# Hybrid decoder layer on one core: block sums of weights in two parts, stores of accumulated tiles from GpSimd's queue, p and x loaded at other steps

## The chip, the core and the metric

The kernel runs on one core of a Trainium2 chip. A core has TensorE (PE, matmuls; its weight loads are listed as PEld), VectorE (DVE), ScalarE (ACT), GpSimd (POOL) and SyncE (SP), each with its own instruction queue in program order, and 16 DMA engines. Here SP issues nearly all DMAs, and POOL issues those that add in flight to a tile. The metric is the device time of one execution in microseconds, and a comparison goes by the median of several.

## What is computed

One decoder layer on x of 1024 x 1024 in float32: half an FFN, two attention mixers with gates, half an FFN, and a gated embedding of p. What matters here:

```python
def rms_norm(x, g):
    xf = x.astype(jnp.float32)
    y = xf * lax.rsqrt(jnp.mean(xf * xf, axis=-1, keepdims=True) + EPS)
    return (y * g.astype(jnp.float32)).astype(x.dtype)

def swiglu(h, w_gate, w_up, w_down):
    return (jax.nn.silu(h @ w_gate) * (h @ w_up)) @ w_down

    x = x + 0.5 * swiglu(rms_norm(x, ffn1_norm[i]), ffn1_w_gate[i], ffn1_w_up[i], ffn1_w_down[i])
    h = rms_norm(x, mix_norm[i])
    ...   # y_fox, y_sb: forgetting and stick-breaking attention on h @ w_in
    merged = (jax.nn.sigmoid(g_fox) * (y_fox @ w_branch_fox[i])
              + jax.nn.sigmoid(g_sb) * (y_sb @ w_branch_sb[i]))
    x = x + merged @ w_out[i]
    x = x + 0.5 * swiglu(rms_norm(x, ffn2_norm[i]), ffn2_w_gate[i], ffn2_w_up[i], ffn2_w_down[i])
    x = x + jax.nn.sigmoid(rms_norm(x, ple_norm[i]) @ w_ple_gate[i]) * (p[i] @ w_ple_proj[i])
```

D_MODEL and SEQ are 1024, D_FF is 2816, PLE_DIM is 256.

## The kernel before

**Products.** Every float32 operand is split into a high and a low part, and a product is three passes (high by high, and the two mixed ones) of four 128-deep matmuls: 12 matmuls of 128x512, all recorded at line 613. `make_up` multiplies the normed activations with weight blocks of 256 columns. Both are cut in two by two, and instead of eight block products it forms seven, of sums and differences, as Strassen's scheme does. Product (n, m) is number m of weight block n. Block 0 alone is done plainly, with eight (`plain`).

**Operands of the weights.** `part(n, m)` names the weight operand of (n, m): four quarters of the two raw tiles `r[0]` and `r[1]`, and sums of them. `sums(n)` (lines 573 to 578) makes three, of 128x512 each, and `last_sum(n)` (line 581) a fourth. `prep(n, m)` splits an operand: ScalarE casts the high part and another engine, VectorE as a rule, subtracts for the low part (line 106 of the helper `split`, the cast is line 105). In the steady blocks POOL makes the sums, at the start of a stage VectorE.

**Operands of the activations.** `combo_a` to `combo_u`, `combo_s`, `combo_d` and `combo_e` form the seven activation operands B[m]; in each, `high` is a cast on ScalarE (line 645) and `low` a subtraction on VectorE (line 649). `combo_s(j, 7)` writes B[7], read by the products (n, 7). `combo_d(j)` (lines 727, 728 or 730) prepares and `combo_e(j)` writes B[4], read by (n, 4). In the first FFN the activations come by rows (`rows()` is true) and each d is two operations.

**Order.** `make_up` is used in four stages: first FFN, gates (in `mix_start`, evictions at lines 1311 to 1325), second FFN, and PLE (`ple_start`, lines 1700 to 1773). Within them the order of each engine's instructions is that of the program text, and a reader waits through semaphores for what it reads or overwrites. Step s of a stage is: product number s of `up_order`, its `evict` from PSUM, `begin(s)`, and `prep` of the product four steps later. The list begins (2,1), (1,5), (2,2), (1,6), (1,7), (2,6), (2,5), (1,3), (2,7), (1,4), (3,1), (2,4), (3,2); PLE, with four blocks, ends (3,6), (3,5), (3,7), (2,3), (3,3), (3,4). Products 1, 6, 7 and 4 of a block add up in one bank of PSUM, and 6 and 7 are each copied out by ScalarE (lines 776 and 778 in the FFNs, 1313 and 1315 in the gates, 1732 and 1734 in PLE). (1,6) and (1,7) are neighbours; in later blocks another product stands between 6 and 7.

**Slots.** Tiles come from tagged slots ("T" six, "Q" two, "KH" two, "WH" three, and so on). A load into a slot waits in its issuing queue until the last reader of the tile before is done.

**PLE.** `pd` holds p @ w_ple_proj and `xe` the residual, both in DRAM. After the sigmoid, `finish(n, i)` multiplies the tile E[n][i] with p's (line 1714), then either POOL issues a DMA that adds x to the tile (line 1716) or VectorE adds a loaded tile of x (line 1718), and the tile is stored (line 1719). `fetch` loads p, or p and x (line 1709). The table `AT` says behind which step each is done.

Of the kernel before, what the change touches and what calls it, by code (L numbers as in the profile page):

```python
# [14 lines left out]
ALU = mybir.AluOpType  # L15
# [3 lines left out]
P = 128  # L19
# [17 lines left out]
def tile_hybrid_decoder_layer(  # L37
# [6 lines left out]
    nc = tc.nc  # L44
# [7 lines left out]
    def nm(s):  # L52
        uid[0] += 1
        return f"{s}_{uid[0]}"

    def slot(tag, shape, dt=F32):
        pad = -shape[-1] % 16
        t = sb.tile([*shape[:-1], shape[-1] + pad], dt, tag=tag, bufs=BUFS[tag], name=nm(tag))
        return t[:, :, :shape[-1]] if pad else t
# [29 lines left out]
    def f(ap):  # L89
        return ap.bitcast(F32)  # L90
# [71 lines left out]
    pd = dp.tile([KD, P, S], F32, name="p_proj")  # L162
# [27 lines left out]
    def norm_sum(N, ps):  # L190

        acc = N.pop("acc")
        for t in range(4):
            pe(nc.tensor.matmul(ps[:, t:t + 1], acc[:, t * P:(t + 1) * P], ones1[:], start=True, stop=True))  # L194
        norm_pow(N, ps)
# [175 lines left out]
    def up_first(N, F):  # L371

        F.load(2)
        F.prep(0, 5)
        F.prep(0, 4)
        F.plain(0, 0, (0, 1), False)
        norm_sum(N[1], bank("sc"))
        F.prep(1, 1)
        F.prep(1, 2)
        F.sums(1, nc.vector)  # L380
        F.silu(0, 0)
        F.prep(1, 5)
        F.plain(1, 0, (0,))
        norm_row(N[1], bank("av"))
        F.plain(1, 0, (1,), False)
        combos(F)
        F.silu(1, 0)
        products(F)
# [144 lines left out]
    def make_up(N, src, nm_, tags, first_fn, first_done=None, over=None):  # L533

        B = {}
        W, hls, E = {}, {}, {}
# [7 lines left out]
        def part(n, m):  # L544
            r = W[n]["r"]
            one, two = slice(0, P), slice(P, 256)
            if m in (6, 7):
                return W[n]["s"][:, 7 - m]
            return {1: r[0][:, :, one], 5: r[0][:, :, two], 2: r[1][:, :, one], 3: r[1][:, :, one], 4: r[1][:, :, two]}[m]

        def plain(f_, half, parts=(0, 1), out=True):

# [17 lines left out]
            if first_done is not None and half:  # L570
                first_done(0, f_, E[0][f_])

        def sums(n, eng=nc.gpsimd):
            W[n]["s"] = slot(tags["sum"].get(n, "RAW"), [P, 2, 4, P])
            a11, a21, a22, s3, s2 = part(n, 1), part(n, 5), part(n, 4), part(n, 7), part(n, 6)
            eng.tensor_sub(s3, a11, a21)
            eng.tensor_add(a21, a21, a22)
            eng.tensor_sub(s2, a21, a11)

        def last_sum(n, eng=nc.gpsimd):  # L580
            eng.tensor_sub(part(n, 2), part(n, 2), part(n, 6))
# [46 lines left out]
        def rows():  # L628
            return "rows" in N[0]
# [95 lines left out]
        def combo_d(j):  # L725
            if rows():
                nc.vector.tensor_sub(w(j, 0), f(cut(B[2], 0, j)), w(j, 1))
                nc.vector.tensor_add(w(j, 0), w(j, 0), f(cut(B[2], 1, j)))
            else:
                nc.vector.tensor_sub(w(j, 0), h0(j, 1), w(j, 1))  # L730

        def combo_e(j):
            if j == 0:
                B[4] = home(4)
            high(4, j, w(j, 0))
            low(4, j, w(j, 0))

        def begin(s):

            if s == 0:  # L740
                for q in range(4):
                    combo_s(q, 7)
            elif s == 1:
                sums(2, nc.vector)
            elif s == 2:
                last_sum(1, nc.vector)
                last_sum(2, nc.vector)
            if rows():
                if 1 < s < 6:
                    combo_d(s - 2)  # L750
            elif 0 < s < 3:
                combo_d(2 * s - 2)
                combo_d(2 * s - 1)
            if 2 < s < 7:
                combo_e(s - 3)
        return types.SimpleNamespace(a=combo_a, b=combo_b, t=combo_t, l=combo_l, u=combo_u, s=combo_s, load=load, prep=prep, sums=sums, last_sum=last_sum, plain=plain, silu=silu, product=product, begin=begin, E=E, B=B, bank_of=bank_of)

    def ffn(N, wg, wu, wd, resid, hid, tags, entry, tail):
# [360 lines left out]
    pend, late = [], []  # L1119
# [489 lines left out]
    tags = {"raw": {1: ("KH", "KL")}, "sum": {}, "w": ("Q", "Q", "KH", "KL"), "hl": ("WL", "WL", "WL", "WH") + ("PT",) * 4 + ("WL", "WL", "WL", "PT"), "B": {"12": "X", 3: ("T",) * 4, 5: "H", 6: "H", 7: "X", 4: "X"}}  # L1609
# [10 lines left out]
    xe = dp.tile([KD, P, S], F32, name="x_end")  # L1620
# [79 lines left out]
    def ple_start():  # L1700

        N, Xs, T = [], [], {}
        tags_p = {"raw": UP_TAGS["raw"], "sum": UP_TAGS["sum"], "hl": UP_TAGS["hl"], "cycle": ("WL", "WL", "WL", "PT", "PT", "PT"),
                  "B": {"12": "H", 3: "H", 5: "X", 6: ("T",) * 4, 7: "H", 4: "X"}}

        def fetch(n, i, *tags):
            r = T[n, i] = [slot(tag, [P, 2, 512]) for tag in tags]
            for t, src in zip(r, (pd, xe)):
                nc.sync.dma_start(t[:], src[2 * n + i].rearrange("p (h n) -> p h n", h=2))

        def finish(n, i, h=slice(0, 2), cols=slice(0, 512), add_in_dma=True):

            e = E[n][i][:, h, cols]
            nc.vector.tensor_mul(e, e, T[n, i][0][:, h, cols])
            if add_in_dma:
                nc.gpsimd.dma_start(e, xe[2 * n + i].rearrange("p (h n) -> p h n", h=2)[:, h, cols], accum_op=ALU.add)
            else:
                nc.vector.tensor_add(e, e, T[n, i][1][:, h, cols])
            nc.sync.dma_start(out[0, (2 * n + i) * P:(2 * n + i + 1) * P, :].rearrange("p (h n) -> p h n", h=2)[:, h, cols], e)

        F = make_up(N, lambda n: kp(w_ple_gate[0])[:, :, n * 256:n * 256 + 256], 4, tags_p, AF.Sigmoid)
        E = F.E
        h0, h1 = slice(0, 1), slice(1, 2)

        def evict(n, m, ps):
            if m == 1:
                E[n] = [slot(t, [P, 2, 512]) for t in (("Y", "Y") if n == 2 else ("GF", "RN"))]
            e1, e2 = E[n]
            if m == 1:
                nc.scalar.copy(e1[:, 0, :], ps[:])  # L1730
            elif m == 6:
                nc.scalar.copy(e1[:, 1, :], ps[:])  # L1732
            elif m == 7:
                nc.scalar.copy(e2[:, 1, :], ps[:])
                nc.vector.tensor_add(e2[:, 1, :], e2[:, 1, :], F.bank_of[n, "d"][:])  # L1735
                nc.scalar.activation(e2[:, 1, :], e2[:, 1, :], AF.Sigmoid)
            elif m == 2:
                nc.vector.tensor_add(e1[:, 0, :], e1[:, 0, :], ps[:])
                if n == 3:
                    nc.scalar.activation(e1[:, 0, :], e1[:, 0, :], AF.Sigmoid)  # L1740
            elif m == 3:
                nc.vector.tensor_add(e1[:, 1, :], e1[:, 1, :], ps[:])
                hs = h1 if n == 3 else slice(0, 2)
                nc.scalar.activation(e1[:, hs], e1[:, hs], AF.Sigmoid)
            elif m == 4:
                nc.scalar.activation(e2[:, 0, :], ps[:], AF.Sigmoid)
        F.evict = evict
        late = (slice(0, 512), False)
        AT = {4: [(fetch, 0, 1, "Q"), (finish, 0, 0)], 6: [(finish, 0, 1), (fetch, 1, 0, "KH"), (fetch, 1, 1, "KH")], 8: [(fetch, 2, 1, "T")],
              9: [(finish, 1, 0)], 10: [(fetch, 3, 0, "Q", "Q")], 11: [(finish, 1, 1), (fetch, 2, 0, "KH", "KH")], 12: [(fetch, 3, 1, "T", "T")],  # L1750
              13: [(finish, 2, 1)], 14: [(finish, 3, 0, h0)], 16: [(finish, 3, 1, h1, *late)], 17: [(finish, 2, 0, slice(0, 2), *late), (finish, 3, 0, h1, *late)]}

        def begin(i, X):
            if not Xs:
                Xs.extend(X)
            up_begin(N, X, 2, F, i)

        def end():
            fetch(0, 0, "T")
            up_first(N, F)  # L1760
            seqn = up_order(4)
            for s, (n, m) in enumerate(seqn[:-1]):
                evict(n, m, F.product(n, m))
                F.begin(s)
                if s + 4 < len(seqn):
                    F.prep(*seqn[s + 4])
                for fn, *args in AT.get(s, ()):
                    fn(*args)
            for cols in (slice(0, 256), slice(256, 512)):
                ps = F.product(3, 4, cols)  # L1770
                nc.scalar.activation(E[3][1][:, 0, cols], ps[:, cols], AF.Sigmoid)  # L1771
                finish(3, 1, h0, cols, False)
        return types.SimpleNamespace(begin=begin, step=lambda i, t: up_step(N, Xs, xe, F, i, t), end=end)
# [36 lines left out]
```

## Time and profile before

| | |
|---|---|
| median of 3 runs | 2266.73 us (2263.55 to 2269.24) |
| the profiled execution | 2264.37 us, span 2262.6 us, granted clock 0.995 |
| PE busy | 2217.6 us, 98% of the span |
| DVE, ACT, POOL busy | 67%, 44%, 36% |
| start of step 0: first FFN, gates, second FFN, PLE | 47.3, 684.8, 1551.7, 2190.2 us |

The page of the profile gives busy times, and beside a group of instructions the idle time just before them and what ended it. In the timeline a row is: start in us, length in us, engine, line, operation, output and inputs by the program's names, count, and in brackets the idle time before it and its releaser. Rows of one kind that follow each other are merged (x24). The ends of matmuls are modelled, so a row of 12 is listed with 2.88 us though the next may start 2.72 us after it. Rows of POOLq and SPq are queues that issue DMAs; the time to landing runs from the issue.

### The profile page before, as it was taken

The page shows a single profiled execution, that of the slowest core. Times are in us where ns is not written, and L with a number is a line of the kernel's source. Part 1 is how long each engine was busy: PE and PEld are TensorE (multiplying, and loading weights), DVE is VectorE, ACT ScalarE, POOL GpSimd, SP SyncE. Part 2 cuts the span into 40 slices and gives each one's busy share as a digit, 9 for nine tenths or more (in the row PEclk, how much of TensorE's full clock was granted, in tenths as well). Part 3 has the DMA queues.
Part 4 walks back from the last instruction along what each step waited for, and adds up shares of the span by engine and source line. Part 5 has one row for each costly group of instructions (what it writes and reads, how often), then busy time and mean ns, then how long its engine had stood idle before and what let it go on. Part 6 is the DMA issues. An engine that isn't in the chain of part 4 may idle for free. (4 is left out here: it accounts for less than half of the span.)

```text
span 2262.6 us, 30509 instructions
## 1 busy us (share of the span) xinstructions
PE 2217.6 (98%) x11210; PEld 1884.4 (83%) x11210; DVE 1511.6 (67%) x2365; ACT 1005.6 (44%) x1805; POOL 817.4 (36%) x788
## 2 busy tenths in 40 slices
PE   9999999999999999999999999999999999999997
PEld 7788888888887899999898888887888888888876
DVE  8755555588887325666678775788554545778895
ACT  6333333333354445555566663255333333433453
POOL 1344444300021336565567664420544444200111
PEclk9999999999999999999999999999999999999998
DMA  4232323384323333233323366641423232754427
GB/s 140 93 126 84 126 80 130 135 320 172 112 93 112 119 119 109 85 113 85 84 66 90 107 196 233 237 162 40 135 93 117 86 124 84 268 197 167 136 69 228
DMA packets 196328, 298.30 MB, mean 132 GB/s; under 512 B 28746, under 2 KB 108874, under 8 KB 196179
## 3 DMA queue, kind: packets, MB, share of 16 engines
q1 hardware_dynamic: 195312, 293.47, 39.1%
q0 software_dynamic: 864, 2.88, 0.8%
q8 instruction: 88, 1.44, 0.3%
q14 instruction: 62, 0.50, 0.1%
q10 hardware_dynamic: 2, 0.00, 0.0%
HBM read 196.40 MB, written 83.13 MB: 124 GB/s over the span
## 5 line engine op out<-in xcount | busy, mean ns | idle before, releaser
L509 PE MATMUL ps<-H,H 128*128 128x512 f32 x2184 | 497.2, 390 | 0.0
L509 PEld LDWEIGHTS ps<-H,H 128*128 128x128 f32 x2184 | 409.8, 188 | 84.5
L613 PE MATMUL ps<-H,WL 128*128 128x512 f32 x1164 | 276.9, 391 | 2.9 <-ACT GF L1732 2.9
L613 PEld LDWEIGHTS ps<-H,WL 128*128 128x128 f32 x1164 | 219.6, 189 | 48.7 <-ACT GF L1732 3.3
L185 POOL TENSOR_TENSOR PT<-PT,PT 128x512 f32<-128x512 f32 x27 | 35.0, 1294 | 405.7 <-ACT PT L182 404.9
L613 PE MATMUL ps<-X,WL 128*128 128x512 f32 (+1 forms) x588 | 140.2, 388 | 12.4 <-ACT RN L1771 9.2
L613 PE MATMUL ps<-H,Q 128*128 128x512 f32 x624 | 148.4, 389 | 0.0
L517 DVE SCALAR_TENSOR_TENSOR X<-ps,X 128x512 f32<-128x512 f32 x168 | 110.2, 686 | 47.4 <-PE ps L509 47.3
L613 PEld LDWEIGHTS ps<-X,WL 128*128 128x128 f32 x588 | 110.1, 191 | 35.0 <-ACT RN L1771 9.4
L613 PEld LDWEIGHTS ps<-H,Q 128*128 128x128 f32 x624 | 117.2, 188 | 24.2
L613 PE MATMUL ps<-H,PT 128*128 128x512 f32 x540 | 129.1, 390 | 0.7 <-DVE RN L1735 0.7
L139 POOL TENSOR_TENSOR WL<-RAW,WH 128x512 fp32r<-128x512 f32 (+1 forms) x84 | 97.4, 1180 | 67.4 <-ACT WH L129 43.2
L1214 DVE TENSOR_TENSOR PT<-ps,PT 128x512 fp32r<-128x512 f32 (+1 forms) x160 | 100.0, 627 | 31.9 <-ACT PT L1208 31.1
L613 PEld LDWEIGHTS ps<-H,PT 128*128 128x128 f32 x540 | 101.3, 188 | 22.1 <-DVE RN L1735 1.1
L891 PE MATMUL ps<-WH,H 128*128 128x256 f32 x768 | 116.2, 288 | 0.8 <-ACT RN L956 0.8
L899 PE MATMUL ps<-H,WH 128*128 128x512 f32 x384 | 115.0, 407 | 0.0
L1232 PE MATMUL ps<-PT,X 128*128 128x256 f32 (+1 forms) x640 | 102.6, 286 | 6.8 <-DVE PT L1214 5.6
L1208 ACT CAST PT<-ps 128x512 fp32r<-128x512 f32 (+1 forms) x160 | 87.1, 548 | 43.1 <-PE ps L1206 40.5
L1232 PEld LDWEIGHTS ps<-PT,X 128*128 128x128 f32 x640 | 90.4, 190 | 17.3 <-DVE PT L1214 10.4
L891 PEld LDWEIGHTS ps<-WH,H 128*128 128x128 f32 x768 | 101.4, 190 | 2.7 <-ACT RN L956 1.2
L412 POOL TENSOR_TENSOR PT<-GF,RN 128x512 f32<-128x512 f32 x20 | 33.6, 1682 | 188.5 <-DVE GF L799 188.5
L1160 POOL TENSOR_TENSOR T<-T,l 128x128 f32<-128x128 f32 (+3 forms) x64 | 73.2, 1146 | 72.5 <-DVE l L1159 70.4
(439 smaller groups left out, 4782.2 us busy)
## 6 DMA issues: line engine op xcount, KB each, us to landing
hidden<-PT SPq DMA_DIRECT2D x40, 512.0 KB, 2.6
WH<-in_ffn_w_gate_dram SPq DMA_DIRECT2D x38, 512.0 KB, 4.9
Q<-hidden SPq DMA_DIRECT2D x24, 512.0 KB, 5.7
hidden<-RN SPq DMA_DIRECT2D x22, 512.0 KB, 2.9
KH<-in_ffn_w_up_dram SPq DMA_DIRECT2D x20, 512.0 KB, 6.2
KL<-in_ffn_w_up_dram SPq DMA_DIRECT2D x20, 512.0 KB, 6.9
T<-in_ffn_w_down_dram SPq DMA_DIRECT2D x20, 512.0 KB, 6.6
GF<-hidden SPq DMA_DIRECT2D x14, 512.0 KB, 7.4
```

What stands on the lines that cost most here:

```text
L139: ins = eng_lo.tensor_sub(lo[part], raw[part], f(hi[part]))
L185: add = lambda eng: eng.tensor_add(N["acc"], N["acc"], d)
L412: eng.tensor_add(s12[:, 0, :], g1[:, 1, :], g2[:, 1, :])
L509: pe(nc.tensor.matmul(groups[g][t][:], wt[:, b, k, t * P:(t + 1) * P], act[:, a, k, :], start=(fresh and n == 0), stop=(i in (6, 1, 4) and ...
L517: nc.vector.scalar_tensor_tensor(xs, groups[g][t][:], scale, xs, ALU.mult, ALU.add)
L613: pe(nc.tensor.matmul(ps[:, cols], hl[:, a, k, :], right(B[m], b, k)[:, cols], start=(first and i == 0), stop=(final and i == 11), skip_gr ...
L891: pe(nc.tensor.matmul(ps[:, :n], hT[t // 4](a, k)[:, (t % 4) * P:(t % 4 + 1) * P], w[k // 4][b][:, k % 4, :n], start=(i == 0), stop=(i == ...
L899: pe(nc.tensor.matmul(ps[:], w[a][:, k, :], hT[half](b, k), start=(i == 0), stop=(i == 23)))
L1160: nc.gpsimd.tensor_mul(T[:, :n], T[:, :n], l[:].broadcast_to([P, n]))
L1208: high = nc.scalar.copy(pt[:, 0, :width], ps[:, :width])
L1214: ins = nc.vector.tensor_sub(pt[:, 1, :width], ps[:, :width], f(pt[:, 0, :width]))
L1232: pe(nc.tensor.matmul(o, lh, r, start=(kpair == c and i == 0), stop=(kpair == 0 and i == 3)))
```

## The change

`sums` now writes a21 + a22 to the first half of a slot and that sum less a11 to the second, and the third sum, a11 - a21, is a function of its own, `third_sum`, done in place in the raw tile. For block 2 the first two are made at step 0 ahead of `combo_s` (all three were made at step 1), the third at step 3, and `last_sum(2)` at step 7 (it was at step 2). Where the rows are not used, d is done at steps 2 and 3 (it was 1 and 2); e is done at steps 4 to 7 everywhere (it was 3 to 6). In PLE a store that follows an adding DMA is issued by POOL and no longer by SP, each `fetch` loads one tile, and the steps and slots of the loads are others.

```diff
@@ make_up
         def part(n, m):
             r = W[n]["r"]
             one, two = slice(0, P), slice(P, 256)
-            if m in (6, 7):
-                return W[n]["s"][:, 7 - m]
-            return {1: r[0][:, :, one], 5: r[0][:, :, two], 2: r[1][:, :, one], 3: r[1][:, :, one], 4: r[1][:, :, two]}[m]
+            if m == 6 or m == 5 and "s" in W[n]:
+                return W[n]["s"][:, m - 5]
+            return {1: r[0][:, :, one], 5: r[0][:, :, two], 7: r[0][:, :, two], 2: r[1][:, :, one], 3: r[1][:, :, one], 4: r[1][:, :, two]}[m]
...
-        def sums(n, eng=nc.gpsimd):
+        def sums(n, eng=nc.gpsimd, split_=False):
+            a21 = part(n, 5)
             W[n]["s"] = slot(tags["sum"].get(n, "RAW"), [P, 2, 4, P])
-            a11, a21, a22, s3, s2 = part(n, 1), part(n, 5), part(n, 4), part(n, 7), part(n, 6)
-            eng.tensor_sub(s3, a11, a21)
-            eng.tensor_add(a21, a21, a22)
-            eng.tensor_sub(s2, a21, a11)
+            eng.tensor_add(part(n, 5), a21, part(n, 4))
+            eng.tensor_sub(part(n, 6), part(n, 5), part(n, 1))
+            if not split_:
+                third_sum(n, eng)
+
+        def third_sum(n, eng):
+            eng.tensor_sub(part(n, 7), part(n, 1), part(n, 7))
...
         def begin(s):

             if s == 0:
+                sums(2, nc.vector, True)
                 for q in range(4):
                     combo_s(q, 7)
-            elif s == 1:
-                sums(2, nc.vector)
             elif s == 2:
                 last_sum(1, nc.vector)
+            elif s == 3:
+                third_sum(2, nc.vector)
+            elif s == 7:
                 last_sum(2, nc.vector)
-            if rows():
-                if 1 < s < 6:
-                    combo_d(s - 2)
-            elif 0 < s < 3:
-                combo_d(2 * s - 2)
-                combo_d(2 * s - 1)
-            if 2 < s < 7:
-                combo_e(s - 3)
+            for j in range(4):
+                if s == (j + 2 if rows() else 2 + j // 2):
+                    combo_d(j)
+            if 3 < s < 8:
+                combo_e(s - 4)
@@ ple_start
-        def fetch(n, i, *tags):
-            r = T[n, i] = [slot(tag, [P, 2, 512]) for tag in tags]
-            for t, src in zip(r, (pd, xe)):
-                nc.sync.dma_start(t[:], src[2 * n + i].rearrange("p (h n) -> p h n", h=2))
+        def fetch(n, i, tag, x=False):
+            t = T[(n, i, "x") if x else (n, i)] = slot(tag, [P, 2, 512])
+            nc.sync.dma_start(t[:], (xe if x else pd)[2 * n + i].rearrange("p (h n) -> p h n", h=2))

         def finish(n, i, h=slice(0, 2), cols=slice(0, 512), add_in_dma=True):

             e = E[n][i][:, h, cols]
-            nc.vector.tensor_mul(e, e, T[n, i][0][:, h, cols])
+            nc.vector.tensor_mul(e, e, T[n, i][:, h, cols])
+            queue = nc.gpsimd if add_in_dma else nc.sync
             if add_in_dma:
-                nc.gpsimd.dma_start(e, xe[2 * n + i].rearrange("p (h n) -> p h n", h=2)[:, h, cols], accum_op=ALU.add)
+                queue.dma_start(e, xe[2 * n + i].rearrange("p (h n) -> p h n", h=2)[:, h, cols], accum_op=ALU.add)
             else:
-                nc.vector.tensor_add(e, e, T[n, i][1][:, h, cols])
-            nc.sync.dma_start(out[0, (2 * n + i) * P:(2 * n + i + 1) * P, :].rearrange("p (h n) -> p h n", h=2)[:, h, cols], e)
+                nc.vector.tensor_add(e, e, T[n, i, "x"][:, h, cols])
+            queue.dma_start(out[0, (2 * n + i) * P:(2 * n + i + 1) * P, :].rearrange("p (h n) -> p h n", h=2)[:, h, cols], e)
...
-        AT = {4: [(fetch, 0, 1, "Q"), (finish, 0, 0)], 6: [(finish, 0, 1), (fetch, 1, 0, "KH"), (fetch, 1, 1, "KH")], 8: [(fetch, 2, 1, "T")],
-              9: [(finish, 1, 0)], 10: [(fetch, 3, 0, "Q", "Q")], 11: [(finish, 1, 1), (fetch, 2, 0, "KH", "KH")], 12: [(fetch, 3, 1, "T", "T")],
-              13: [(finish, 2, 1)], 14: [(finish, 3, 0, h0)], 16: [(finish, 3, 1, h1, *late)], 17: [(finish, 2, 0, slice(0, 2), *late), (finish, 3, 0, h1, *late)]}
+        AT = {4: [(finish, 0, 0)], 5: [(fetch, 2, 1, "T")], 6: [(finish, 0, 1), (fetch, 1, 0, "Q"), (fetch, 1, 1, "Q"), (fetch, 3, 0, "KH"), (fetch, 3, 0, "KH", True)],
+              7: [(fetch, 3, 1, "T")], 9: [(finish, 1, 0)], 10: [(fetch, 3, 1, "Q", True)], 11: [(finish, 1, 1)], 12: [(fetch, 2, 0, "Q")],
+              13: [(finish, 2, 1)], 14: [(finish, 3, 0, h0), (fetch, 2, 0, "T", True)], 16: [(finish, 3, 1, h1, *late)], 17: [(finish, 2, 0, slice(0, 2), *late), (finish, 3, 0, h1, *late)]}
...
         def end():
             fetch(0, 0, "T")
+            fetch(0, 1, "T")
             up_first(N, F)
```

## The prediction

> **What bounds the kernel now.** I read the busy line of the page, then the waits of PE, then the timeline where those waits lie, then SP's and POOL's queues at the end.
>
> ```profile
> PE 2217.6 (98%) x11210; PEld 1884.4 (83%) x11210; DVE 1511.6 (67%) x2365; ACT 1005.6 (44%) x1805; POOL 817.4 (36%) x788
> ...
> PE ps L613 <- ACT RN L1771: 9.2, 1, 9.2
> PE ps L613 <- ACT Y L776: 6.1, 2, 3.2
> ...
> PE ps L613 <- ACT GF L1313: 2.9, 1, 2.9
> PE ps L613 <- ACT GF L1732: 2.9, 1, 2.9
> ...
> PE ps L613 <- DVE RN L1735: 0.7, 1, 0.7
> ```
>
> PE is the bound, so only its idle time and what lies behind its last matmul can be won. Five of its waits lie in code that the change touches. Four are one place in four stages (first FFN, gates, second FFN, PLE): product (1,7) waits for ScalarE's copy of (1,6). The fifth, 9.2 us, is the last half product. The PLE stage shows the first kind, by timeline and then by windows (length, busy time of PE, PEld, DVE, ACT and POOL with counts, granted clock, DMA share, GB/s):
>
> ```profile
> 2196.19 0.69 DVE L106 TENSOR_TENSOR WL<-WH,WL 128x512 fp32r<-128x512 f32 x1 [0.31 <-ACT WL L105]
> 2197.19 1.29 DVE L649 TENSOR_TENSOR H<-Q,H 128x512 fp32r<-128x512 f32 x2 [0.31 <-ACT H L645]
> 2198.31 2.88 PE L613 MATMUL ps<-T,WL 128*128 128x512 f32 x12
> 2202.38 0.62 ACT L105 CAST PT<-KL 128x512 fp32r<-128x512 f32 x1 [3.14 <-DVE KL L578]
> 2203.42 0.58 ACT L1732 COPY GF<-ps 128x512 f32<-128x512 f32 x1
> 2204.05 4.36 PE L613 MATMUL ps<-H,WL 128*128 128x512 f32 x12 [2.86 <-ACT GF L1732]
> 2208.25 2.90 PE L613 MATMUL ps<-T,PT 128*128 128x512 f32 x12
> 2213.71 5.60 PE L613 MATMUL ps<-H,WL 128*128 128x512 f32 x24
> 2219.15 2.88 PE L613 MATMUL ps<-X,PT 128*128 128x512 f32 x12
> 2222.07 0.60 ACT L1746 ACTIVATE RN<-ps 128x512 f32<-128x512 f32 x1 [0.24 <-PE ps L613]
> ```
> ```profile
> 2204.00:2206.00 2.00, 1.95 (x5) 1.56 (x6) 2.00 (x5) 0.00 (x0) 0.00 (x0) 0.50 0.00 0
> ```
>
> The copy is free to run when (1,6) ends, but it stands in ScalarE's queue behind the cast for (2,6), which waits for the third of VectorE's block sums, which stand behind four low parts (L649) and one prep. Then PE restarts at a clock of 0.50. A product normally takes 2.72 (half of 2219.15 - 2213.71). So the place costs 2204.05 - 2198.31 - 2.72 = 3.02 and then 2208.25 - 2204.05 - 2.72 = 1.48. The other three stages:
>
> ```profile
> 52.74 5.60 PE L613 MATMUL ps<-H,WL 128*128 128x512 f32 x24
> 61.50 3.04 PE L613 MATMUL ps<-X,WL 128*128 128x512 f32 x12 [3.16 <-ACT Y L776]
> 64.38 2.88 PE L613 MATMUL ps<-H,PT 128*128 128x512 f32 x12
> ...
> 693.00 2.88 PE L613 MATMUL ps<-T,WL 128*128 128x512 f32 x12
> 698.75 2.08 PE L613 MATMUL ps<-T,WL 128*128 128x512 f32 x4 [2.87 <-ACT GF L1313]
> 702.96 2.88 PE L613 MATMUL ps<-T,PT 128*128 128x512 f32 x12
> ...
> 1557.09 5.60 PE L613 MATMUL ps<-H,WL 128*128 128x512 f32 x24
> 1565.61 4.43 PE L613 MATMUL ps<-T,WL 128*128 128x512 f32 x12 [2.92 <-ACT Y L776]
> 1569.88 2.88 PE L613 MATMUL ps<-H,PT 128*128 128x512 f32 x12
> ```
>
> Read alike (two products of 2.72 in the x24 rows): first FFN 3.32 + 0.16, gates 3.03 + 1.49, second FFN 3.08 + 1.55. The first FFN kept its clock.
>
> **The change part by part.**
>
> *Block sums in two parts, earlier.* The count of VectorE operations is unchanged; they move. At step 0 two sums go ahead of the four L649. VectorE is free at about 2196.9 (end of the 2196.19 row), so both sums are done near 2198.3, the lows near 2200.7, the low half of (1,7) near 2201.3; at 0.6 to 0.7 each. ScalarE's cast for (2,6) no longer waits, and its copy starts when (1,6) ends. What stays is the copy itself: 2.88 + 0.04 (start of ScalarE behind PE's end) + 0.58 + 0.05 = 3.55 from the start of (1,6), so 0.83 more than a product. The 0.04 is the distance in the 2219.15 and 2222.07 rows. (1,7) would start at 2201.86; its operands are there at 2201.3. An idle of 0.8 should not lower the clock: behind the 0.7 wait on L1735 the product took 3.04, not 4.36 (the 2241.79 row below). Gain: 2.49 + 0.16 in the first FFN, 2.20 + 1.49, 2.25 + 1.55, 2.19 + 1.48: 13.8 in all. Bounds: nothing of it, or 17.1 were the copy hidden too; I take 13.8, as the copy has a row.
>
> [...]
>
> *Third sum, last_sum and the d and e combinations later.* The e's write the operand of (1,4) (step 9); the last one moves from step 6 to step 7, behind the eviction of (1,3). Followed op by op with the same durations, VectorE in gates and second FFN finishes it before the matmul that reads it (the eighth of the product for the low part, 1.6 us in). In the first FFN each d is two operations and the eviction ends in a 1.2 us multiply: the last low comes about 1.6 too late. In PLE two multiplies and a sigmoid stand ahead:
>
> ```profile
> 2212.18 1.22 DVE L1714 TENSOR_TENSOR GF<-GF,T 128x1024 f32<-128x1024 f32 x1
> 2216.86 0.68 DVE L1742 TENSOR_TENSOR GF<-GF,ps 128x512 f32<-128x512 f32 x1
> 2217.57 1.06 ACT L1744 ACTIVATE GF<-GF 128x1024 f32<-128x1024 f32 x1 [3.55 <-DVE GF L1742]
> ```
>
> There the last high part comes near 2217.6 where PE wants it at 2216.1: 1.5. So 3.1 goes back; bounds 0 and 2.6 per stage (were the whole of the operand awaited before the first matmul). Net per stage: 1.0, 3.7, 3.8, and 2.2 in PLE; 8.5 before PLE.
>
> The release of the raw tile moves from the prep of (n,5) to that of (n,7), so block 3's first load leaves at step 0 and not early; before, SP stood at the second one until 2205 anyway, and the use lies at step 6. Priced at nothing; without that cover it would cost a load of about 4 us. last_sum(2) goes from step 2 to 7, two steps (5.4 us) ahead of its use in the FFNs and gates, more in PLE: nothing, as VectorE has caught up by then; with no such slack it would cost its 0.7. In the steady blocks the three sums stay where they are and only change order, each three or more products ahead of its use: nothing; were POOL late there, (n,7) would wait for one sum of 1.3 (the L581 row below) more.
>
> *Loads sooner, stores from POOL.* The end before, SP and engines, and the DMA issues:
>
> ```profile
> 2240.09 0.58 SPq L1709 DMA_DIRECT2D T<-x_end  x1
> 2241.79 3.04 PE L613 MATMUL ps<-H,PT 128*128 128x512 f32 x12 [0.72 <-DVE RN L1735]
> 2251.96 0.69 DVE L1714 TENSOR_TENSOR RN<-RN,T 128x512 f32<-128x512 f32 x1 [9.62 <-DMA T<-p_proj]
> 2253.83 0.68 DVE L1742 TENSOR_TENSOR GF<-GF,ps 128x512 f32<-128x512 f32 x1
> ```
> ```profile
> GF<-x_end POOLq DMA_DIRECT2D x2, 512.0 KB, 5.4
> ...
> Y<-x_end POOLq DMA_DIRECT2D x1, 512.0 KB, 9.5
> ...
> out_dram<-GF SPq DMA_DIRECT2D x2, 256.0 KB, 2.1
> GF<-x_end POOLq DMA_DIRECT2D x1, 256.0 KB, 7.7
> ```
>
> SP issues in order: a store waits for its accumulation, the loads of block 3 stand behind it, the last is issued at 2240.09, VectorE waits 9.62, and the sigmoid that PE waits for comes later still. Now p(0,1) is loaded at the stage's start, when SP has nothing due but block 2's weights, and it delays those by the 0.5 of an issue. At step 6 SP waits for slots that the e's free, the last near 2218; behind that wait stand only the loads for the last block and block 2, used 15 us and more later. With the loads at steps 5 to 14 and no dependent store in SP's queue, this wait and the 0.72 go. The last eviction L1742 would start 0.04 behind (3,3), which ends at 2241.79 + 2.88 - 0.72 - 2.2 = 2241.75; from L1742 to the end of the span it took 2262.6 - 2253.8 = 8.8 of VectorE work and a store. VectorE's end: 2250.6.
>
> But POOL now issues an accumulation, waits for its landing, issues the store, and only then the next accumulation:
>
> ```profile
> 2213.97 1.06 POOL L1716 DMA_DIRECT2D GF<-x_end  x1 [35.92 <-ACT X L645]
> 2217.47 0.87 POOL L1716 DMA_DIRECT2D RN<-x_end  x1 [2.44 <-DVE RN L1714]
> 2223.40 1.28 POOL L581 TENSOR_TENSOR WH<-WH,KL 128x512 f32<-128x512 f32 x1 [5.06 <-DVE WL L106]
> ```
>
> Before, the second left 3.5 behind the first, with the first in flight. A pair now takes 5.4 + 0.9 = 6.3 (issue of a store taken as that of an accumulation). Six pairs, the last of half size, start near 2211.7 (the first multiply moves up 2.2): 5 x 6.3 + 1.3 (last_sum(3) between) + 4.0 + 0.9 + 2.1 gives 2251.5 at best (4.0 for half an accumulation is an estimate between 2.7, half of 5.4, and 5.4). The first two run beside the loads of steps 5 to 7; the row for an accumulation among six loads is 9.5, so 0 to 4.1 more each; I take 2.0 and 1.5, as three or four fall together: 2255.0. last_sum(3) is delayed to about 2228, its use lies near 2231; ScalarE's copy into the slot of the first stored tile (step 10) waits for that store as before, and (3,6), which needs it, comes 5 us later. So POOL's queue is what comes last: PLE ends 7.6 earlier, not 12.0.
>
> [...]
>
> **Sum.** 8.5 + 7.6 = 16.1. The profiled execution took 2264.37, 2.4 under the median of the runs (2266.73); from the one it gives 2248.3, from the median 2250.6, which I predict.
>
> **The rivals.** *VectorE's end sets the time*: accumulations land in 5.4 or less beside the loads. 8.5 + 12.0 = 20.5: 2246.2. For it: the 5.4 rows; against: by these POOL still ends 0.9 later.
>
> *The deferred e's give the stage gains back*: the last e late by 2.6 in all four stages, or the clock falls again at the 0.8 and 1.5 stalls. The stages before PLE keep 2 instead of 8.5: 2257.1. For it: VectorE is all but unbroken through steps 0 to 7; against: the slack found in gates and second FFN.
>
> *The loads are sooner in the program, not on the chip*: SP stands at the slot that the last e frees, the loads crowd again, and the end keeps its place. Only 8.5: 2258.2. Against: the slot is free near 2218, and the last eviction comes more than 20 us later.
>
> *Slower: POOL's queue.* Every accumulation takes 9.5 as Y's did, a pair 10.4: 2211.7 + 52 + 1.3 + 7.7 + 3.0 = 2275.7, 13.1 later than before, which with 8.5 gained in the other stages is 4.6 over the median, 2271.3. It decides from 9.5 a pair; beyond 10.8 the kernel is slower by over 0.3%. For it: the 9.5 and 7.7 rows; against: those ran beside six loads of blocks 2 and 3, and most of the six will not.
>
> **How the numbers follow.** Forecast 0.42, VectorE's end 0.22, e's 0.18, loads 0.08, POOL's queue 0.10. About 0.3% (6.8 us) is what a measurement of this kernel can tell from no change. Faster: 0.42 + 0.22 + most of the e's 0.14 + 0.04 = 0.82; within: 0.04 + 0.04 + half of POOL's, 0.13; slower 0.05. Range 2243 to 2263: from VectorE's end with the copies cheaper to the e's and loads cases with the spread of the runs. The forecast's own range is 2247 to 2256.
>
> **What would show it.** Right: the four waits on the copy of (1,6) near 0.8 and the next product near 2.9; a wait or gap inside (1,4) in the first FFN and PLE of about 1.5; no wait on L1771 over 2; SP without waits on accumulations; POOL's accumulations 6 to 9 apart and the last store POOL's. Wrong: a copy still behind a cast, a clock of 0.50 after it, (1,4) late in all stages, or VectorE's stores last.

## The result and the profile after

The changed kernel takes 2258.99 us in the median (2257.09 to 2260.29, 18 runs), the kernel before 2265.45 (2260.91 to 2269.24, 18 runs, the first three among them): a ratio of 0.9972, 95% interval 0.9965 to 0.9979. It is 6.5 us faster where 16.1 were forecast, and lies outside the forecast's own range of 2247 to 2256. The profiled execution took 2257.49, with a span of 2255.8 (before: 2262.6).

The line numbers have moved: the matmuls are now at 617, the cast of `high` at 649, the subtraction of `low` at 653, PLE's multiply at 1716, its accumulation at 1719, its stores at 1722. PE's waits in the parts that the change touches, from the view of waits (total, times, longest):

```profile
PE ps L617 <- DVE X L653: 2.0, 1, 2.0
PE ps L617 <- ACT Y L779: 1.3, 2, 0.7
...
PE ps L617 <- ACT GF L1316: 0.7, 1, 0.7
PE ps L617 <- ACT GF L1735: 0.7, 1, 0.7
PE ps L617 <- ACT X L649: 0.6, 1, 0.6
...
PE ps L617 <- ACT RN L1775: 0.5, 1, 0.5
```

All four waits on the copy of (1,6) are 0.7 now, and the 9.2 at the end is 0.5. Two gaps are new, inside (1,4): 2.0 in the first FFN and 0.6 in PLE. The opening of PLE in the timeline:

```profile
2192.36 0.58 ACT L1735 COPY GF<-ps 128x512 f32<-128x512 f32 x1 [1.17 <-PE ps L617]
2192.99 3.01 PE L617 MATMUL ps<-H,WL 128*128 128x512 f32 x12 [0.68 <-ACT GF L1735]
2195.84 2.88 PE L617 MATMUL ps<-T,PT 128*128 128x512 f32 x12
```

The copy waits for PE and no longer for a cast, and the product behind it is near its full pace (2195.84 - 2192.99 = 2.85, of which 0.13 are the restart). (1,6) of PLE starts at 2189.44 against 2198.31: 8.87 us ahead, where 8.5 were forecast. So PLE begins as early as forecast, and yet the end is only 6.8 earlier. The end, in POOL's timeline and in the last of SP's:

```profile
2202.97 1.07 POOL L1719 DMA_DIRECT2D GF<-x_end  x1 [34.02 <-DVE X L653]
2212.99 0.59 POOL L1722 DMA_DIRECT2D out_dram<-GF  x1 [8.95 <-DMA GF<-x_end]
2213.60 0.89 POOL L1719 DMA_DIRECT2D RN<-x_end  x1
2221.89 0.56 POOL L1722 DMA_DIRECT2D out_dram<-RN  x1 [7.40 <-DMA Q<-x_end]
2223.69 0.96 POOL L1719 DMA_DIRECT2D GF<-x_end  x1
2231.71 0.56 POOL L1722 DMA_DIRECT2D out_dram<-GF  x1 [7.06 <-DVE RN L1716]
2232.27 0.90 POOL L1719 DMA_DIRECT2D RN<-x_end  x1
2238.11 1.12 SPq L1722 DMA_DIRECT2D out_dram<-RN  x2
2239.46 0.58 POOL L1722 DMA_DIRECT2D out_dram<-RN  x1 [6.29 <-DMA RN<-x_end]
2240.17 0.87 POOL L1719 DMA_DIRECT2D Y<-x_end  x1
2246.63 0.56 POOL L1722 DMA_DIRECT2D out_dram<-Y  x1 [5.59 <-DMA Y<-x_end]
2247.27 0.88 POOL L1719 DMA_DIRECT2D GF<-x_end  x1
2252.29 0.57 POOL L1722 DMA_DIRECT2D out_dram<-GF  x1 [4.14 <-DMA GF<-x_end]
```

Each pair of rows is one accumulation and the store that waits for it; no accumulation starts before the store ahead. VectorE and SP have issued everything by 2239.2; POOL goes on alone for 13 us. From the first accumulation to the end of the span it is 52.8 us. The accumulations, from their issue to the issue of their store, take 10.0, 8.3, 8.0, 7.2, 6.5 and, the last of half size, 5.0; forecast were 7.4, 6.9, 5.4, 5.4, 5.4 and 4.0.

### The profile page after: what moved, and what is told of

Same layout as the page of the kernel before. It is cut to its first block, busy times and chain, and to the rows that moved or that the text cites. A ratio compares the mean times of both kernels' runs of the same rounds, so it can differ in the third digit from the quotient of the medians.

```text
span 2255.8 us, 30537 instructions
## 1 busy us (share of the span) xinstructions
PE 2213.0 (98%) x11210; PEld 1879.2 (83%) x11210; DVE 1507.5 (67%) x2365; ACT 1005.5 (45%) x1805; POOL 823.3 (36%) x794
## 5 line engine op out<-in xcount | busy, mean ns | idle before, releaser
L1235 PEld LDWEIGHTS ps<-PT,X 128*128 128x128 f32 x640 | 90.3, 190 | 17.2 <-DVE PT L1217 10.4
```

What stands on the lines that cost most here:

```text
L1235: pe(nc.tensor.matmul(o, lh, r, start=(kpair == c and i == 0), stop=(kpair == 0 and i == 3)))
```

## The experiments

The theory after the trace: the openings are worth what was forecast, and POOL's serial queue takes it back at the end, the more as each accumulation is slow. The rival: the transfers at the end need that long whoever issues them (the DMA engines are 83 to 94% busy in the windows of the first four accumulations).

**Only the block sums and combinations.** PLE's loads, slots and stores are those of before.

```diff
+ part, sums, third_sum and begin of the changed kernel
  fetch, finish and AT of the kernel before
```

> The kernel before with the part of the change in the block sums and combinations alone; loads and stores of PLE as before. Theory P (the openings of the stages gain as the trace of the changed kernel shows, and POOL's serial queue gives part of it back at the end): 8.65 us ahead of PLE and about 2.3 in its opening, so about 11 us less than before, 2254 to 2255, that is faster than the whole change. The PE waits on the copies 0.7 each. If the openings do not add to the end (rival Q, the transfers at the end need their time whoever issues them): 5 to 7 us less, no better than the whole change.

2254.61 us, ratio 0.9952 (0.9940 to 0.9965): 11.0 less than before, as P expected, and 4.4 faster than the whole change. The rival Q is out. The four waits on the copies are 0.7 each, and the old end is still there:

```profile
PE ps L617 <- ACT RN L1774: 9.3, 1, 9.3
...
PE ps L617 <- DVE X L653: 1.9, 1, 1.9
```

So this half of the change carries all of the gain.

**Only PLE's loads and stores.**

```diff
  part, sums and begin of the kernel before
+ fetch, finish and AT of the changed kernel
```

> The kernel before with the change of loads, slots and store queues in PLE alone. P: POOL's chain from the first accumulation to the end of the span lasts about 52.8 us as in the changed kernel; it starts near 2213 to 2214, so the span is about 2266, some 3 to 4 us SLOWER than before. Q: the loads are sooner and the transfers end with them: 4 to 10 us faster than before.

2272.3 us, ratio 1.0026 (1.0015 to 1.0037): slower than before by 6.6 in the medians (5.9 by the ratio), more than the 3 to 4 expected. POOL's chain:

```profile
2216.03 1.07 POOL L1716 DMA_DIRECT2D GF<-x_end  x1 [36.21 <-DVE X L649]
...
2267.08 0.57 POOL L1719 DMA_DIRECT2D out_dram<-GF  x1 [4.31 <-DMA GF<-x_end]
```

With a span of 2270.6 the chain is 54.6 us long, 1.8 more than the 52.8 expected, and it starts 2 to 3 us later than expected. Of that, 1.8 arise ahead of PLE, which starts at 2191.92 here and at 2190.15 before, though the program ahead of PLE is the same. An estimate: had the product behind the wait in the first FFN run as slowly here as that behind the wait in PLE, 4.62 us, and not in the 3.04 it took before, that would be 1.6 of the 1.8; the mean granted clock, 0.993 here and 0.995 before, agrees. The other half of the change is a loss.

**All stores from SP's queue again,** the loads as changed.

```diff
-            queue = nc.gpsimd if add_in_dma else nc.sync
+            queue = nc.sync
```

> The changed kernel with all stores of PLE issued by SP, the accumulations still by POOL. P: POOL no longer waits, accumulations start when their tiles are ready; SP stands behind the first accumulation for 6 to 8 us and delays the loads, yet the end is VectorE's: span 2241 to 2247, 8 to 14 us less than the changed kernel. Q: the same bytes, the same end: within 3 us of the changed kernel.

2251.86 us, ratio 0.9940 (0.9927 to 0.9952): 7.1 less than the changed kernel. The rival's same end is refuted; the gain is smaller than expected, as SP's order now delays the loads:

```profile
2202.93 1.06 POOL L1719 DMA_DIRECT2D GF<-x_end  x1 [34.00 <-ACT X L649]
2206.43 0.87 POOL L1719 DMA_DIRECT2D RN<-x_end  x1 [2.43 <-DVE RN L1716]
2208.55 0.36 SPq L1722 DMA_DIRECT2D out_dram<-GF  x1
2209.01 0.44 SPq L1711 DMA_DIRECT2D T<-p_proj  x1
2238.83 1.23 DVE L1716 TENSOR_TENSOR Y<-Y,Q 128x1024 f32<-128x1024 f32 x1 [5.06 <-DMA Q<-p_proj]
2243.21 1.22 DVE L1721 TENSOR_TENSOR Y<-Y,T 128x1024 f32<-128x1024 f32 x1 [3.16 <-DMA T<-x_end]
```

The second accumulation leaves 3.5 behind the first. The first has landed when SP issues its store, 5.6 after the issue and not 10.0: the loads stand behind that store and do not run beside it. Then the late loads cost VectorE 5.06 and 3.16.

**Each POOL store behind the next accumulation.**

```diff
                 nc.gpsimd.dma_start(e, xe[...], accum_op=ALU.add)
...
+            stores()                    # issues what is pending
+            pending.append((dst, e))
...
+ 15: [(stores,)]
```

> The changed kernel with each of POOL's stores issued behind the next accumulation, not ahead of it (the last one a step after its accumulation). P: two accumulations overlap, POOL's last store lands near 2240 to 2244, the span ends with VectorE's stores or just behind, 2241 to 2246, 10 to 14 us less than the changed kernel. Q: the accumulations only run longer beside each other, the end stays within 4 us of the changed kernel.

2247.94 us, ratio 0.9923 (0.9910 to 0.9937): 11.0 less than the changed kernel, with the same bytes from the same queue. The rival is out. What is new is a wait of PE:

```profile
2203.20 1.08 POOL L1719 DMA_DIRECT2D GF<-x_end  x1 [34.04 <-DVE X L653]
2206.66 0.89 POOL L1719 DMA_DIRECT2D RN<-x_end  x1 [2.38 <-DVE RN L1716]
2213.30 0.57 POOL L1731 DMA_DIRECT2D out_dram<-GF  x1 [5.74 <-DMA GF<-x_end]
2220.34 0.58 ACT L1742 COPY GF<-ps 128x512 f32<-128x512 f32 x1 [7.91 <-DMA out_dram<-GF]
2220.98 4.27 PE L617 MATMUL ps<-T,WL 128*128 128x512 f32 x12 [2.10 <-ACT GF L1742]
2240.49 0.56 POOL L1731 DMA_DIRECT2D out_dram<-GF  x1 [2.75 <-DMA GF<-x_end]
```

Two accumulations overlap and last longer each (median from issue to landing 9.2 us for GF and 9.5 for RN, 8.7 and 7.4 in the changed kernel), but POOL's last store leaves at 2240.5 and not 2252.3. Block 3's tile takes the slot of the first stored tile, and ScalarE waits for that store to land.

**What makes an accumulation slow.** First the bytes of the stores are taken away, then the loads.

```diff
+            if add_in_dma:
+                dst, e = dst[:, 0:1, 0:128], e[:, 0:1, 0:128]
```

> The changed kernel, but each store behind an accumulation writes only a 128x128 piece (64 KB of 512; the rest of those output tiles is left out): order and waits of POOL stay, the bytes do not. Theory S (the accumulations last long because the store ahead of them in POOL's queue is still moving): the five accumulations behind a store fall towards 5.5, the first stays at 10; POOL's chain of 52.8 us falls by 6 to 9, the span by as much. Theory L (the loads beside them do it): the first three stay at 8 to 10, the later ones fall by 1 at most; the span falls by 2 to 4, most of it from the last store's landing and the last two accumulations.

2253.61 us. From the first accumulation to the end it is 48.6 us, 4.2 less than in the changed kernel. By POOL's timeline the accumulations take 10.1, 7.5, 6.1, 5.7, 7.1 and 4.7: the first stays, the second loses 0.8, the third and fourth lose 1.9 and 1.5, and Y's takes 0.6 longer. Neither S (five near 5.5, a chain 6 to 9 shorter) nor L (at most 1 less each) describes this alone.

The chain starts 1.7 later than in the changed kernel, as PLE does (2182.99 against 2181.28), so the span (2253.3) is only 2.5 shorter.

```profile
2204.69 1.07 POOL L1719 DMA_DIRECT2D GF<-x_end  x1 [34.01 <-DVE X L653]
2214.81 0.60 POOL L1725 DMA_DIRECT2D out_dram<-GF  x1 [9.04 <-DMA GF<-x_end]
```

```diff
+            if n:
+                T[(n, i, "x") if x else (n, i)] = T[0, 1]
+                return
```

> The changed kernel without PLE's loads of p and x for blocks 1 to 3 (the tile of p(0,1) stands in for all of them, so those outputs are of other data; the same operations, the stores whole). L: the first accumulation falls from 10.0 to 5.4, the second and third from 8 to 6 to 6.5; chain 52.8 less 7 to 9, span 2247 to 2249. S: only the first falls, the span by 4 to 5 us.

2249.23 us, and the chain is 44.6 us, 8.2 less than in the changed kernel:

```profile
2202.91 1.07 POOL L1722 DMA_DIRECT2D GF<-x_end  x1 [34.02 <-DVE X L653]
2208.82 0.59 POOL L1725 DMA_DIRECT2D out_dram<-GF  x1 [4.85 <-DMA GF<-x_end]
...
2244.01 0.57 POOL L1725 DMA_DIRECT2D out_dram<-GF  x1 [4.71 <-DMA GF<-x_end]
```

The first accumulation takes 5.9 where it took 10.0, the second 6.4 for 8.3, the third 5.6 for 8.0, as L expected. So the loads are the larger part (8.2) and the stores' own bytes a smaller one (4.2, of which 0.4 lie behind the issue of the last store). Both at once were not taken away, so the two need not add. The loads leave from SP's queue and the accumulations from POOL's, and still the first accumulation took 10.0 with them and 5.9 without.

**The e combinations a step earlier,** as before the change.

```diff
-            if 3 < s < 8:
-                combo_e(s - 4)
+            if 2 < s < 7:
+                combo_e(s - 3)
```

> The changed kernel with the four e combinations a step earlier, steps 3 to 6, as before the change. My theory (the deferral costs the 2.0 us gap inside (1,4) in the first FFN and 0.6 in PLE): both gaps go, no new wait, 2 to 3 us less than the changed kernel. Rival (VectorE is full, the work only delays something else): the gaps turn into waits at (2,5), (1,3) or (2,7), within 0.7 us of the changed kernel.

2258.5 us, against 2258.99 for the changed kernel, so within 0.7. But not by the rival's way: both gaps are gone, and no wait at (2,5), (1,3) or (2,7) came. (1,4) in the first FFN, in PE's timeline, and a wait in PLE that is new:

```profile
73.33 2.88 PE L617 MATMUL ps<-X,Q 128*128 128x512 f32 x12
...
2219.28 4.36 PE L617 MATMUL ps<-T,WL 128*128 128x512 f32 x12 [2.99 <-ACT GF L1733]
```

POOL's first and last rows:

```profile
2202.89 1.07 POOL L1719 DMA_DIRECT2D GF<-x_end  x1 [35.42 <-DVE X L653]
...
2253.95 0.57 POOL L1722 DMA_DIRECT2D out_dram<-GF  x1 [4.29 <-DMA GF<-x_end]
```

PE reaches PLE 1.5 sooner, but POOL's first accumulation starts no sooner (VectorE has one e more ahead of the multiply for it, which starts at 2201.07 against 2201.15) and its chain is 54.6 us, so what PE won came to nothing at the end. The new wait, on ScalarE's copy into the slot of the first stored tile, also takes 3.0 of PE and slows the product behind it; with POOL ending last it does not show in the time. My expectation for the time was wrong because it left POOL's chain out, and "no new wait" was wrong too.

**Towards a faster kernel.** First the late stores, with slots of their own for block 3:

```diff
-                E[n] = [... ("Y", "Y") if n == 2 else ("GF", "RN") ...]
+                E[n] = [... ("Y", "Y") if n == 2 else ("KL", "WH") if n == 3 else ("GF", "RN") ...]
```

> The kernel with POOL's stores one accumulation later, and the tiles of block 3 in slots of their own, so that ScalarE's copy at step 10 does not wait for the first store. If the 2.1 us wait of PE on that copy and the slow product behind it (4.27 instead of 2.9) come from the slot: both go, 3 to 3.6 us less than with the late stores alone (2247.9), 2244 to 2245. If the end is set by the landing of the last stores anyway: within 1 us of it.

2245.41 us, ratio 0.9910 (0.9896 to 0.9924). The 2.1 wait on the copy is gone and the slow product with it, and 2.5 of the 3 to 3.6 arrived. Then with the e's early too:

> Late stores, block 3 in slots of its own, and the e combinations a step earlier (steps 3 to 6). If the earlier e's were without effect on the changed kernel only because POOL's chain set the end: here their 2.0 us in the first FFN and 0.6 in PLE come through, 2242 to 2243.5 against 2245.4 without. If VectorE is full and gives them back: 2245 to 2246.

2243.23 us, ratio 0.9902 (0.9886 to 0.9919): the e's bring 2.2 here, which brought nothing where POOL set the end. Last, one accumulation less:

```diff
-  14: [(finish, 3, 0, h0), ...]
+  14: [(finish, 3, 0, h0, *late), ...]
```

> As the run before, and the first half of the tile (3,0) gets its x from VectorE (the loaded tile, at step 14) and is stored by SP, so one accumulation of 256 KB and one store of POOL are gone. If the last stores' landing beside the accumulations sets the end: 1 to 2 us less than the run before, 2240.5 to 2242. If VectorE's chain to the last store does: the same within 0.7 us.

2242.26 us, ratio 0.9898 (0.9883 to 0.9912): 1.0 less again, at the lower edge of the 1 to 2 and above the rival's 0.7, so this last step tells the two only weakly. It is 16.7 less than the changed kernel.

## Why the prediction was wrong

The step that failed is the term "POOL's chain" under *Loads sooner, stores from POOL*: the mechanism was named, its size was not. From the first accumulation to the end I had 2255.0 - 2211.7 = 43.3 us; it measured 52.8. That is 9.5 more, and the chain started 0.2 earlier than the sum had it; together this is the whole miss, 16.1 against 6.8 in the span. By pair, from accumulation to accumulation, the 9.5 are 2.3, 1.0, 2.3, 1.6 and 0.8, then 1.0 in the last half accumulation and 0.5 from the last store to the end.

- **The loads beside the accumulations.** I took 2.0 and 1.5 for the first two and nothing for the rest. Taking the loads away showed 8.2 over the chain. The row of 9.5 was the right one for the first (10.0), not something to halve: SP issued four loads at 2202.4 to 2204.2 and two more near 2209, so six had left before it landed, as many as beside the row of 9.5.
- **The bound called "at best" was none.** Even with the loads away the chain is 44.6, where I had 2251.5 - 2211.7 = 39.8. Of the difference 2.7 lie in the five pairs, 1.6 in the half accumulation (5.6 there, 5.0 in the changed kernel, not 4.0) and 0.5 behind the last store. The 5.4 was measured with no store just ahead of the accumulation, and here four of the five whole ones have their predecessor's store in flight and take 5.6 to 7.0. That the store does it is shown beside the loads (small stores), not without them.
- **The chances.** The rival in which POOL's queue makes the kernel slower rests on the same term. A pair took (2247.27 - 2202.97 - 1.3) / 5 = 8.6, between my 7.0 (6.3, with the 2.0 and 1.5 spread over five) and its 10.4; from 9.5 on the kernel would have been slower. With PLE's part alone, at 8.9 a pair and without the gain ahead of PLE, it was slower.
- **Rivals that come near by number.** The rivals of 2257.1 (deferred e's) and 2258.2 (loads) lie nearer to the measured 2258.99 than the forecast does, but neither is what happened: the e's cost two gaps and not four, and VectorE's end did move, to 2239.
- **Block sums.** Right in the openings: waits of 0.7, the clock at 1.00 behind them. The three slow restarts went with the long waits, which the run with the sums alone shows too. That 8.87 were won ahead of PLE for 8.5 is in part luck. From the start of one stage to the next, the first FFN won 0.4 (forecast 1.0), the opening of the gates 3.55 (3.7) and the second FFN 3.65 (3.8), 7.6 in all. Another 1.6 came between the gates and the second FFN, in shorter waits of code that the change doesn't touch, for which I know no cause, and the first FFN began 0.35 later.
- **The deferred e's.** Right in place, 2.0 for 1.6 in the first FFN and 0.6 for 1.5 in PLE. In the first FFN the activations come by rows, and the fifth matmul, not the eighth, needs the last low part. That in PLE was smaller: the last high part was there 1.45 behind the start of (1,4), where I had counted about 2.1.
- **SP and VectorE's end.** Right: SP waits for no accumulation, the wait on L1771 is 0.5, SP's last stores are issued by 2239.2. Moved by the 8.87, my 2250.6 for the end of these stores is 2241.7, and they do land near it (3.1 from issue to landing); had nothing else been left, this would have been the rival of 2246.2. The late stores came to 2247.9, and with what they uncovered mended, the e's early and one accumulation less, 2242.3.
- **The copy into the slot of the first stored tile.** I gave it 5 us of slack. It had none, since the first accumulation took 10.0: in the changed kernel the weight load waited 0.43 (row below) and the product started 0.2 late. With the late stores PE waited 2.10, as the store itself took 7.0 to land there (2213.30 to 2220.34) beside the second and third accumulation, against 5.1.

```profile
2218.06 0.59 ACT L1733 COPY GF<-ps 128x512 f32<-128x512 f32 x1 [5.84 <-DMA out_dram<-GF]
2218.70 2.60 PEld L617 LDWEIGHTS ps<-T,WL 128*128 128x128 f32 x12 [0.43 <-ACT GF L1733]
```

## What to carry to other kernels

A wait for a transfer, put into a queue which starts other transfers, made the chain accumulate, land, store, accumulate serial here, 52.8 us from its first accumulation to the end; before, another queue held that wait. Move the dependent issue one turn later, behind the next independent one, and keep the queue: here that alone was worth 11 us. Price a transfer by the row taken beside as much traffic as it will have in flight until it lands, not by the emptiest (here by 9.5 and not 5.4, for a first accumulation that took 10.0), and when a gain upstream does not arrive, look at which queue issues last.

## What the runs showed of the hardware

The first accumulating transfer of 512 KB took 5.9 us, to the issue of its store, with the loads away, and 10.0 beside six loads of the same size. In the changed kernel POOL issued a plain store in 0.56 to 0.59 and an accumulation in 0.87 to 1.07 us; I had taken 0.9 for both.

In these runs the clock of PE behind an idle time isn't told by its length alone. Behind 2.10 us a product took 4.27 (late stores), behind about 2.9 it took 4.2 to 4.4 (before), yet behind 3.16 in the first FFN it took 3.04. The 2.0 gap in the changed kernel left it alone:

```profile
73.10 1.07 PE L617 MATMUL ps<-X,Q 128*128 128x512 f32 x4
76.14 2.11 PE L617 MATMUL ps<-X,Q 128*128 128x512 f32 x8 [1.97 <-DVE X L653]
```

Eight matmuls in 2.11 are at full pace, and the granted clock is 1.00 there. In the run with the block sums alone the same gap is 1.91 long, and there the clock falls behind it. PE's rows and the granted clock (third number from the end of a window) of that run:

```profile
75.96 2.92 PE L617 MATMUL ps<-X,Q 128*128 128x512 f32 x8 [1.91 <-DVE X L653]
```
```profile
73.64:77.05 3.41, 1.50 (x7) 0.90 (x6) 3.41 (x6) 0.13 (x1) 0.00 (x0) 1.00 0.55 198
77.00:80.00 3.00, 3.00 (x9) 2.34 (x8) 2.96 (x6) 1.67 (x3) 0.28 (x1) 0.51 0.00 0
80.00:81.00 1.00, 1.00 (x5) 0.82 (x4) 1.00 (x2) 0.00 (x0) 1.00 (x2) 0.77 0.00 0
```

From these rows the clock is at 0.50 from about 77.05 to 80.46, near 3.4 us long, and it falls 1.1 us after PE has restarted. In the kernel before it falls at 698.26, 1565.24 and 2203.53, there 0.49, 0.37 and 0.52 us ahead of the restart, and stays at 0.50 for 3.41 us each time; behind the 3.16 in the first FFN it stays at 1.00:

```profile
61.00:65.00 4.00, 3.50 (x15) 2.91 (x16) 3.97 (x8) 1.11 (x3) 0.00 (x0) 1.00 0.00 0
698.26:701.67 3.41, 2.92 (x7) 2.34 (x8) 3.41 (x6) 0.44 (x1) 0.00 (x0) 0.50 0.13 13
1565.25:1568.65 3.40, 3.04 (x7) 2.46 (x8) 3.40 (x7) 0.31 (x1) 0.00 (x0) 0.50 0.19 20
2203.54:2206.94 3.40, 2.89 (x7) 2.31 (x8) 3.40 (x7) 0.46 (x1) 0.00 (x0) 0.50 0.10 31
```

So behind gaps of 1.9 to 3.2 us the clock fell in some places and not in others, and the longest of them kept it. What decides it, no run here was made to tell.
